# Sparse layer of a hybrid block: the key and value compression in halves between gate, value and query products, its second layer later, and the residual scaled inside the attention

## The chip, the cores and the metric

The kernel runs on one core of a Trainium2 chip. The metric is the device time of one execution in microseconds (us). Before the change it is 1653.73 us, the median of 3 runs (1653.6 to 1656.01).

## The reference

The program is a stack on 512 tokens of width 1024, all in float32. A first block (a pooling mixer and an mLSTM) ends with `rms_norm(h, norm_out_g)`. A second block of two layers follows. Its first layer is a sparse attention (NSA), the second a sliding-window attention; each is followed by a gated feed-forward part. The change lies in the sparse layer, after its input `h = rms_norm(x, norm_mix[0])`:

```python
q, kc, vc, ks, vs, kw, vw, gt = split(h @ w_in)     # 16 query heads, 4 key/value groups, head size 64
# q, kc, ks, kw are rotated (rope)
blk = (t[:, :, cidx] + pe).reshape(b, g, 31, 32 * 64)   # 31 overlapping blocks of 32 tokens
c   = gelu(blk @ w1) @ w2                               # compress: 2048 -> 256 -> 64, for kc and for vc
o_cmp = softmax(q @ compressed_keys) @ compressed_values
o_slc, o_win = attention on ks, vs and on kw, vw        # with 512 tokens both see all earlier tokens
o = gate0 * o_cmp + gate1 * o_slc + gate2 * o_win       # gates = sigmoid(gt + gate_b)
x = x + o @ w_o
```

The `x` of the last line is the output of the first block's norm, so it is the raw sum times a factor per token and a gain per feature; the kernel scales its residual tile `H` by both at some point before `w_o` adds to it.

## The kernel before

Activations lie transposed: features on the 128 partitions, 512 tokens along the free dimension, eight chunks for the width of 1024. `H` [128, 8, 512] holds the residual.

A float32 product is made of three matmuls in a faster 32-bit type. `split_into` and `unit` make of each operand a high half (a cast on ScalarE, ACT: `xh`, `wh`) and a low half (what is left, a subtraction on VectorE, DVE: `xl`, `wl`), and `mm3` multiplies high by high, high by low and low by high. `linear` takes one 512 KB piece of weights (128 output columns): `raw` loads it on the SyncE queue (SP) into one of three buffers `wr`, `unit` casts it (L120) and subtracts (L121) into one of three `wh` and three `wl`, and 8 x 3 matmuls (L126 to L128) fill one PSUM bank of 512 columns. The gate product has 48 output columns and 192 KB. The PSUM banks are two `mm`, three `S`, two `tp` and one `po`; with `wide=True` a product takes them in rotation, all but `tp`.

The compression's first layer is different: its weights come by `raw` too, eight pieces of 512 KB (four for keys, four for values), but are used in float32 as they are (L993). TensorE (PE) runs each of the 32 matmuls of one compression as two instructions on 124 columns, so the trace has 64.

The sparse layer (`nsa`) goes like this in program order:
1. the input is split, the first three products (`pre`) run beside the norm's sum of squares, and the rotation tables are scaled;
2. `cproj(0)` and `cproj(1)` evacuate the products for compressed keys and values (`cf`; keys are rotated), and `cmp_blocks` adds the position term into the block tiles `blk` (L981; per compression 12 additions on DVE and 4 on GpSimd, POOL);
3. `kproj(0)`: two key products, rotated by `rope` (a copy L601 on ACT, four small DMAs on SP that swap halves, `rot`, a product on POOL L606, a product and a sum on DVE L607, L608, into `kf`), then `dup_k`: scaled high and low halves and their copies into the other 64 partitions (L615 to L618, ACT and DVE);
4. `compress` of the keys: first layer L993 into two PSUM tiles, copies to `gx` on ACT (L998), the tanh form of gelu in five DVE instructions and one of ACT, second layer L1008 on PE, and two evacuations into `bd`; then `compress` of the values likewise, with the second layer L1015 and `vbd`;
5. `settle`: the norm's factor is broadcast over partitions (L190 on PE, a copy on ACT into `r1`), and eight DVE instructions (L817) scale `H` by it and by the gain;
6. `gate_proj`, `vproj(0)` (two products, evacuated to `vT`, transposed back by L644 in `v_nat`), `qproj(0)`, `cprobs(0)` (softmax on compressed keys), `qproj(1)`, `cvals(0)`;
7. the attention `att(fill)`: 32 steps, head pair p of 8 times query block j of 4. A step first runs what `fill` has for it (further projections, compressed softmax, output products), then the softmax of the step after (`nsa_soft`: scores on PE, maximum L929 or L938 on DVE, exponential L942 on ACT, and the scaling by the gates on DVE L955, POOL L953 and ACT L951), then the values of its own (`nsa_vals`: transposes L662, splits L148 and L149, products L666, L667).

The tiles `cf`, `kf`, `gt`, `vT`, `r1` and `qf` share two buffers of one tag ("kf"), so each waits until the one before the last is released.

The lines above give the program order. The framework (Tile) derives all waits from the tiles, and plans the order of each engine's queue before the run: of the instructions that its own estimate takes as ready, the one that is earliest in the program goes first. On the chip each engine, and SP with its DMA issues, then takes its queue strictly in that order.

Of the kernel before, what the change touches and what calls it, by code (L numbers as in the profile page):

```python
# [11 lines left out]
F32 = mybir.dt.float32  # L12
# [4 lines left out]
OP = mybir.AluOpType  # L17
# [4 lines left out]
T = 512  # L22
NT = 4
KC = 8
# [5 lines left out]
POOL_WINDOWS = (2, 4, 8, 16)  # L30

# [4 lines left out]
class Model:  # L36
    def __init__(self, ctx, tc, a, out):
# [4 lines left out]
        self.wpool = False  # L42
        con = self.con = ctx.enter_context(tc.tile_pool(name="con", bufs=1))
# [12 lines left out]
    def first_loads(self):  # L56
# [7 lines left out]
        r = self.wp.tile([128, 1024], F32, name=self.n("wr"), tag="wr", bufs=3)  # L64
# [39 lines left out]
    def wide_ps(self, shape=(128, 512)):  # L104

        self.rot_ps = (self.rot_ps + 1) % 6
        return (self.mm_ps, self.s_ps, self.s_ps, self.mm_ps, self.s_ps, self.o_ps)[self.rot_ps](shape)

    def raw(self, dram, i, cols=1024):
        r = self.wp.tile([128, 1024], F32, name=self.n("wr"), tag="wr", bufs=3)  # L110
        self.nc.sync.dma_start(r[:, :cols], dram[i])
        return r
# [572 lines left out]
    def nsa(self):  # L685
        tc, nc, a = self.tc, self.nc, self.a
        V, G, S, PE = nc.vector, nc.gpsimd, nc.scalar, nc.tensor
        with tc.tile_pool(name="nsa", bufs=1) as ap:
# [20 lines left out]
            X = {}  # L709
# [24 lines left out]
            def vproj(hf, wide=False):  # L734
                for b in range(2):
                    ps = self.linear(a["nsa_w"], 6 + 8 * hf + b, xh, xl, wide=wide)
                    vT = ap.tile([128, T], F32, name=self.n("vT"), tag="kf", bufs=2)
                    V.tensor_tensor(vT, ps, rb, op=OP.mult)
                    VV[b, hf] = self.v_nat(ap, vT, f"vn{b}", 1)

# [60 lines left out]
            def gate_proj():  # L801
# [3 lines left out]
                V.tensor_scalar(gt, gt, self.v("nsa_gate_b")[:48], None, op0=OP.add)  # L805
                gp = self.tp_ps([128, NT, 48])
# [4 lines left out]
                V.reciprocal(gn, gn)  # L811

            def settle():
                r1 = ap.tile([128, T], F32, name="r1", tag="kf", bufs=2)
                self.bcast(y1, r1)
                for k in range(KC):
                    V.scalar_tensor_tensor(self.H[:, k, :], self.H[:, k, :], self.v("norm_out_g", k), r1,  # L817
                                           op0=OP.mult, op1=OP.mult)

            bk = cproj(0)  # L820
            bv = cproj(1)
            kproj(0, True)
            self.compress(ap, 0, bk, w2, bd, vbd)
            self.compress(ap, 1, bv, w2, bd, vbd)
            settle()
            gate_proj()
            vproj(0, True)
            qproj(0, True)
            cprobs(0)
            qproj(1)  # L830
# [3 lines left out]
            add = lambda p, j, f, *x: fill.setdefault(4 * p + j, []).append(L(f, *x))  # L834
            add(0, 1, cprobs, 1)
# [13 lines left out]
            add(4, 0, vproj, 1)  # L849
# [134 lines left out]
    def compress(self, pool, kv, blk, w2, bd, vbd):  # L984
        nc, a = self.nc, self.a
        V, S, PE = nc.vector, nc.scalar, nc.tensor
        hps = [self.wide_ps([128, 124]) for _ in range(2)]
        for q in range(4):
            w = self.raw(a["cmp_w1"], 4 * kv + q)
            for jj in range(4):  # L990
                j = 4 * q + jj
                for m in range(2):
                    PE.matmul(hps[m], w[:, jj * 256 + m * 128:jj * 256 + m * 128 + 128], blk[j // 8][:, j % 8, :],  # L993
                              start=(j == 0), stop=(j == 15))
        x = pool.tile([128, 2, 124], F32, name=self.n("gx"), tag="pc", bufs=2)
        t = pool.tile([128, 2, 124], F32, name=self.n("gt_"), tag="pc", bufs=2)
        for m in range(2):
            S.copy(x[:, m], hps[m])  # L998
# [5 lines left out]
        V.tensor_scalar(x, x, 0.5, None, op0=OP.mult)  # L1004
        if kv == 0:
# [5 lines left out]
        else:  # L1011
# [5 lines left out]
            for h in range(2):  # L1017
                V.tensor_copy(vbd[32 * h:32 * h + 31, :, h * 64:h * 64 + 64], ps)

# [408 lines left out]
```

## Time and profile before

| | |
|---|---|
| median of 3 runs | 1653.73 us (1653.6 to 1656.01) |
| the profiled execution's own time | 1655.41 us |
| its span, first to last instruction | 1653.7 us, granted TensorE clock 0.992 |
| busy: PE, DVE, ACT, POOL | 1604.0, 1076.7, 790.6, 226.3 us |
| HBM read over the span | 130.50 MB, 80 GB/s |

The profile shows one execution. Busy times are the instructions' own durations; PE's are pipelined, and a matmul's end is modelled, so start-to-start times tell more than durations. "Granted clock" is the share of the full TensorE clock (2.4 GHz) that was granted; 0.50 is 1.2 GHz. In a timeline a row gives the start, the length and the group of instructions that follow each other; in brackets stands the idle time of the engine before it and what ended that. The sparse layer takes 384 to 750 us of the span; its part up to the first attention step ends near 488 us.

### The profile page before, as it was taken

The page shows a single profiled execution, that of the slowest core. Times are in us where ns is not written, and L with a number is a line of the kernel's source. Part 1 is how long each engine was busy: PE and PEld are TensorE (multiplying, and loading weights), DVE is VectorE, ACT ScalarE, POOL GpSimd, SP SyncE. Part 2 cuts the span into 40 slices and gives each one's busy share as a digit, 9 for nine tenths or more (in the row PEclk, how much of TensorE's full clock was granted, in tenths as well). Part 3 has the DMA queues.
Part 4 walks back from the last instruction along what each step waited for, and adds up shares of the span by engine and source line. Part 5 has one row for each costly group of instructions (what it writes and reads, how often), then busy time and mean ns, then how long its engine had stood idle before and what let it go on. Part 6 is the DMA issues. An engine that isn't in the chain of part 4 may idle for free.

```text
span 1653.7 us, 21346 instructions
## 1 busy us (share of the span) xinstructions
PE 1604.0 (97%) x7860; PEld 1302.9 (79%) x7860; DVE 1076.7 (65%) x1878; ACT 790.6 (48%) x1520; POOL 226.3 (14%) x294
## 2 busy tenths in 40 slices
PE   8999999999799999999999999998999999999998
PEld 6678888878677777777888888886777888888886
DVE  7677557766779999986555445357988655534532
ACT  5443265644248887764333233145876433323412
POOL 0000000142212212121111001013311111100100
PEclk9999999999899999999999999999999999999999
DMA  5222321133331111113323333233321323232321
GB/s 183 71 90 90 99 81 42 49 97 102 120 102 46 35 62 39 52 33 109 102 90 101 97 95 102 76 116 94 108 74 60 103 95 102 90 101 90 124 80 51
DMA packets 44792, 142.77 MB, mean 86 GB/s; under 512 B 6608, under 2 KB 6864, under 8 KB 44688
## 3 DMA queue, kind: packets, MB, share of 16 engines
q1 hardware_dynamic: 42384, 137.45, 26.7%
q10 hardware_dynamic: 2304, 3.96, 0.7%
q8 instruction: 62, 1.02, 0.3%
q14 instruction: 42, 0.34, 0.1%
HBM read 130.50 MB, written 2.10 MB: 80 GB/s over the span
## 4 chain that ended last, share of the span: by engine, by line
PE 81%; DVE 11%; ACT 4%; issue 3%; POOL 0%; DMA 0%; DVEq 0%; POOLq 0%; ACTq 0%
PE S L126 10%; PE S L128 10%; PE S L127 10%; PE mm L126 9%; PE mm L127 9%; PE mm L128 9%; PE po L126 3%; PE po L127 3%; PE po L128 3%; PE tp L662 2%; PE po L666 1%; PE po L667 1%; DVE wl L121 1%; DVE blk L981 1%; DVE ptl L149 1%
## 5 line engine op out<-in xcount | busy, mean ns | idle before, releaser
L120 ACT CAST wh<-wr 128x1024 fp32r<-128x1024 f32 (+1 forms) x224 | 233.1, 1043 | 486.4 <-PE S L127 208.4
L121 DVE TENSOR_TENSOR wl<-wr,wh 128x1024 fp32r<-128x1024 f32 (+1 forms) x215 | 264.6, 1231 | 51.2 <-ACT wh L120 35.9
L126 PE MATMUL mm<-xh,wh 128*128 128x512 f32 (+1 forms) x568 | 226.4, 399 | 0.7 <-ACT xh L148 0.4
L127 PE MATMUL mm<-xl,wh 128*128 128x512 f32 (+1 forms) x568 | 225.2, 396 | 0.5 <-DVE xl L152 0.5
L128 PE MATMUL mm<-xh,wl 128*128 128x512 f32 (+1 forms) x568 | 224.8, 396 | 0.0
L126 PE MATMUL S<-xh,wh 128*128 128x512 f32 x520 | 203.9, 392 | 7.1 <-ACT wh L69 6.4
L127 PE MATMUL S<-xl,wh 128*128 128x512 f32 x520 | 203.6, 392 | 0.7 <-DVE xl L152 0.5
L128 PE MATMUL S<-xh,wl 128*128 128x512 f32 x520 | 203.2, 391 | 0.2 <-DVE wl L121 0.2
L126 PEld LDWEIGHTS mm<-xh,wh 128*128 128x128 f32 (+1 forms) x568 | 106.8, 188 | 22.2 <-ACT xh L148 0.9
L127 PEld LDWEIGHTS mm<-xl,wh 128*128 128x128 f32 (+1 forms) x568 | 106.6, 188 | 22.1 <-DVE xl L152 1.2
L128 PEld LDWEIGHTS mm<-xh,wl 128*128 128x128 f32 (+1 forms) x568 | 106.6, 188 | 21.0 <-DVE wl L121 0.4
L126 PEld LDWEIGHTS S<-xh,wh 128*128 128x128 f32 x520 | 97.9, 188 | 28.2 <-ACT wh L69 6.4
L127 PEld LDWEIGHTS S<-xl,wh 128*128 128x128 f32 x520 | 98.0, 188 | 23.0 <-DVE xl L152 2.8
L128 PEld LDWEIGHTS S<-xh,wl 128*128 128x128 f32 x520 | 98.0, 189 | 21.2 <-DVE wl L121 1.3
L149 DVE TENSOR_TENSOR ptl<-tp,pth 128x512 fp32r<-128x512 f32 (+1 forms) x112 | 73.7, 664 | 7.0 <-ACT pth L148 6.2
L942 ACT ACTIVATE p<-S,nm 128x128 f32<-128x128 f32 (+3 forms) x128 | 67.3, 534 | 10.4 <-DVE nm L938 5.1
L148 ACT CAST pth<-tp 128x512 fp32r<-128x512 f32 (+1 forms) x112 | 63.3, 575 | 18.7 <-PE tp L662 15.9
L126 PE MATMUL po<-xh,wh 128*128 128x512 f32 x184 | 71.8, 390 | 0.0
L127 PE MATMUL po<-xl,wh 128*128 128x512 f32 x184 | 71.7, 390 | 0.0
L128 PE MATMUL po<-xh,wl 128*128 128x512 f32 x184 | 71.6, 389 | 0.0
L1201 POOL MEMSET fa<- 128x2 f32 x44 | 4.3, 100 | 450.6 <-DVE fc L1206 449.4
L1207 ACT ACTIVATE fc<-fc 128x512 f32<-128x512 f32 x44 | 27.9, 634 | 78.8 <-DVE fc L1206 78.8
(469 smaller groups left out, 3534.5 us busy)
## 6 DMA issues: line engine op xcount, KB each, us to landing
wr<-ffn_gu SPq DMA_DIRECT2D x88, 512.0 KB, 3.5
wr<-w_in SPq DMA_DIRECT2D x32, 512.0 KB, 3.7
wr<-ffn_d SPq DMA_DIRECT2D x32, 512.0 KB, 3.5
wr<-nsa_w SPq DMA_DIRECT2D x20, 512.0 KB, 3.6
wr<-w_out SPq DMA_DIRECT2D x16, 512.0 KB, 3.5
rot<-sq SPq DMA_DIRECT2D x92, 64.0 KB, 2.0
wr<-swa_w SPq DMA_DIRECT2D x10, 512.0 KB, 3.5
wr<-cmp_w SPq DMA_DIRECT2D x8, 512.0 KB, 4.2
```

Source lines behind the costliest of these rows:

```text
L120: nc.scalar.copy(h[:, :cols], r[:, :cols])
L121: (nc.gpsimd if self.wpool else nc.vector).tensor_tensor(l[:, :cols], r[:, :cols], h[:, :cols], op=OP.subtract)
L126: mm(ps, wh, xh, start=first, stop=False)
L127: mm(ps, wh, xl, start=False, stop=False)
L128: mm(ps, wl, xh, start=False, stop=last)
L148: nc.scalar.copy(h, src)
L149: nc.vector.tensor_tensor(l, src, h, op=OP.subtract)
L662: self.nc.tensor.transpose(ps[:, x, h, :], srcs[x][h], self.ident)
L666: self.nc.tensor.matmul(o, v, ph, start=first, stop=False)
L667: self.nc.tensor.matmul(o, v, pl, start=False, stop=last)
L942: S.activation(t[:, :w], sb[b], AF.Exp, bias=nm[:, 0, h, b:b + 1], accum_out=nm[:, 1, h, b:b + 1])
L1207: S.activation(c, c, AF.Silu)
```

## The change

- A fourth buffer for raw weights (`WR = 4`), everywhere in the kernel.
- In the sparse layer the rotation of wide PSUM banks leaves out `po` until the first `cprobs` (`self.banks = 5`).
- `compress` becomes a generator with a stop after each quarter of its first layer (16 of the trace's 64 instructions), after the gelu and after the second layer. Both column halves go into one `po` bank (one copy to `gx` instead of two), and `gx` and its scratch get a tag of their own.
- `vproj` does one product and is a generator (product and evacuation; transposes), `gate_proj` too (product and evacuation; transposes and sigmoid).
- They are advanced in this order: two key quarters, gate product, two key quarters with gelu, value product 0, gate transposes, two value quarters, value product 1, transposes of 0, two value quarters with gelu, second layer for keys, query product 0, transposes of 1, broadcast of `r1`, query product 1, second layer for values, then `cprobs(0)` and `cvals(0)`.
- `settle` scales one chunk of `H`, as a multiplication by the gain on ACT and one by `r1` on POOL. The eight calls stand in `fill` at the steps j = 1 and 3 of head pairs 0 to 3. `r1` has its own tile.
- The later `vproj(1)` is advanced as product, product, transposes, transposes in step (4, 0).

```diff
+WR = 4
...
     def wide_ps(self, shape=(128, 512)):
 
-        self.rot_ps = (self.rot_ps + 1) % 6
+        self.rot_ps = (self.rot_ps + 1) % self.banks
...
     def raw(self, dram, i, cols=1024):
-        r = self.wp.tile([128, 1024], F32, name=self.n("wr"), tag="wr", bufs=3)
+        r = self.wp.tile([128, 1024], F32, name=self.n("wr"), tag="wr", bufs=WR)
...
-            X = {}
+            self.banks = 5
...
-            def vproj(hf, wide=False):
-                for b in range(2):
+            def vproj(hf, b, wide=False):
+                if True:
                     ps = self.linear(a["nsa_w"], 6 + 8 * hf + b, xh, xl, wide=wide)
                     vT = ap.tile([128, T], F32, name=self.n("vT"), tag="kf", bufs=2)
                     V.tensor_tensor(vT, ps, rb, op=OP.mult)
+                    yield
                     VV[b, hf] = self.v_nat(ap, vT, f"vn{b}", 1)
+                    yield
...
                 V.tensor_scalar(gt, gt, self.v("nsa_gate_b")[:48], None, op0=OP.add)
+                yield
                 gp = self.tp_ps([128, NT, 48])
...
-            def settle():
-                r1 = ap.tile([128, T], F32, name="r1", tag="kf", bufs=2)
-                self.bcast(y1, r1)
-                for k in range(KC):
-                    V.scalar_tensor_tensor(self.H[:, k, :], self.H[:, k, :], self.v("norm_out_g", k), r1,
-                                           op0=OP.mult, op1=OP.mult)
+                yield
+
+            def settle(k):
+                S.mul(self.H[:, k, :], self.H[:, k, :], self.v("norm_out_g", k))
+                G.tensor_tensor(self.H[:, k, :], self.H[:, k, :], r1, op=OP.mult)
 
             bk = cproj(0)
             bv = cproj(1)
             kproj(0, True)
-            self.compress(ap, 0, bk, w2, bd, vbd)
-            self.compress(ap, 1, bv, w2, bd, vbd)
-            settle()
-            gate_proj()
-            vproj(0, True)
+            ck = self.compress(ap, 0, bk, w2, bd, vbd)
+            cv = self.compress(ap, 1, bv, w2, bd, vbd)
+            gt = gate_proj()
+            v0, v1 = [vproj(0, b, True) for b in range(2)]
+            next(ck)
+            next(ck)
+            next(gt)
+            next(ck)
+            next(ck)
+            next(v0)
+            next(gt)
+            next(cv)
+            next(cv)
+            next(v1)
+            next(v0)
+            next(cv)
+            next(cv)
+            next(ck)
             qproj(0, True)
+            next(v1)
+            r1 = ap.tile([128, T], F32, name="r1")
+            self.bcast(y1, r1)
+            qproj(1, True)
+            next(cv)
+            self.banks = 6
             cprobs(0)
-            qproj(1)
             cvals(0)
...
+            for k in range(KC):
+                add(k // 2, 1 + 2 * (k % 2), settle, k)
...
-            add(4, 0, vproj, 1)
+            v2, v3 = [vproj(1, b) for b in range(2)]
+            for g in (v2, v3, v2, v3):
+                add(4, 0, next, g)
...
     def compress(self, pool, kv, blk, w2, bd, vbd):
         nc, a = self.nc, self.a
         V, S, PE = nc.vector, nc.scalar, nc.tensor
-        hps = [self.wide_ps([128, 124]) for _ in range(2)]
+        hps = self.o_ps([128, 2, 124])
         for q in range(4):
             w = self.raw(a["cmp_w1"], 4 * kv + q)
             for jj in range(4):
                 j = 4 * q + jj
                 for m in range(2):
-                    PE.matmul(hps[m], w[:, jj * 256 + m * 128:jj * 256 + m * 128 + 128], blk[j // 8][:, j % 8, :],
-                              start=(j == 0), stop=(j == 15))
-        x = pool.tile([128, 2, 124], F32, name=self.n("gx"), tag="pc", bufs=2)
-        t = pool.tile([128, 2, 124], F32, name=self.n("gt_"), tag="pc", bufs=2)
-        for m in range(2):
-            S.copy(x[:, m], hps[m])
+                    PE.matmul(hps[:, m], w[:, jj * 256 + m * 128:jj * 256 + m * 128 + 128], blk[j // 8][:, j % 8, :],
+                              start=(j == 0 and m == 0), stop=(j == 15 and m == 1))
+            if q < 3:
+                yield
+        x, t = [pool.tile([128, 2, 128], F32, name=self.n(s), tag="gx", bufs=2)[:, :, 0:124] for s in ("gx", "gt_")]
+        S.copy(x, hps)
...
         V.tensor_scalar(x, x, 0.5, None, op0=OP.mult)
+        yield
...
                 V.tensor_copy(vbd[32 * h:32 * h + 31, :, h * 64:h * 64 + 64], ps)
+        yield
```

## Rows read from the trace of the kernel before

**Rows 1.** The page's first part: busy us of each engine, its share of the span and its instructions.

```profile
PE 1604.0 (97%) x7860; PEld 1302.9 (79%) x7860; DVE 1076.7 (65%) x1878; ACT 790.6 (48%) x1520; POOL 226.3 (14%) x294
```

**Rows 2.** Busy time by stretch: from and to in us, length, busy us of PE, PEld (its weight loads), DVE, ACT and POOL with instructions in brackets, granted clock, DMA share, GB/s.

```profile
405.00:420.00 15.00, 15.00 (x72) 12.55 (x71) 12.14 (x16) 2.23 (x3) 6.19 (x6) 1.00 0.27 79
420.00:450.00 30.00, 20.50 (x139) 19.15 (x138) 21.07 (x34) 8.78 (x17) 5.92 (x6) 0.84 0.35 113
450.00:480.00 30.00, 29.88 (x157) 22.99 (x157) 20.49 (x30) 10.77 (x15) 0.00 (x0) 0.99 0.44 140
...
560.00:610.00 50.00, 49.28 (x293) 38.77 (x292) 48.60 (x99) 42.38 (x104) 12.04 (x14) 1.00 0.23 69
```

**Rows 3.** Timeline of PE from 423 to 460 us: start, length, line, result and operands, count, and the wait before it.

```profile
423.70 0.38 PE L993 MATMUL po<-blk,wr 128*128 128x124 f32 x2
...
430.96 0.48 PE L993 MATMUL po<-blk,wr 128*128 128x124 f32 x2 [1.75 <-DMA wr<-cmp_w]
...
433.02 3.83 PE L993 MATMUL S<-blk,wr 128*128 128x124 f32 x32
437.94 0.46 PE L993 MATMUL S<-blk,wr 128*128 128x124 f32 x2 [1.09 <-DMA wr<-cmp_w]
445.05 1.19 PE L1008 MATMUL tp<-gx,w 128*128 128x124 f32 x4 [6.65 <-DVE gx L1004]
446.03 5.78 PE L993 MATMUL S<-blk,wr 128*128 128x124 f32 x30
451.57 0.47 PE L126 MATMUL mm<-xh,wh 128*48 128x512 f32 x1
...
454.70 1.05 PE L1015 MATMUL tp<-w,gx 128*31 128x64 f32 x16
455.68 1.16 PE L190 MATMUL tp<-ident,nwy 128*128 128x128 f32 x8
...
459.46 0.39 PE L126 MATMUL S<-xh,wh 128*128 128x512 f32 x1
```

**Rows 4.** Busy time in stretches of 2 us, columns as in rows 2; the granted clock is the number after POOL.

```profile
439.00:441.00 2.00, 0.00 (x0) 0.00 (x0) 1.37 (x2) 1.94 (x4) 0.00 (x0) 0.88 0.12 44
...
447.00:449.00 2.00, 2.00 (x11) 2.00 (x11) 0.45 (x1) 0.00 (x0) 0.00 (x0) 0.50 0.00 0
449.00:451.00 2.00, 2.00 (x13) 2.00 (x12) 0.00 (x0) 0.00 (x0) 0.00 (x0) 0.56 0.32 63
```

**Rows 5.** Timeline of DVE from 413 to 447 us.

```profile
413.69 8.26 DVE L981 TENSOR_TENSOR blk<-cf,pe 64x248 f32<-64x248 f32 x12
...
423.19 9.78 DVE L981 TENSOR_TENSOR blk<-cf,pe 64x248 f32<-64x248 f32 x12
...
434.20 0.68 DVE L608 TENSOR_TENSOR kf<-kf,rot 128x512 f32<-128x512 f32 x1
435.58 1.40 DVE L616 SCALAR_TENSOR_TENSOR kd<-kf,kd 64x512 fp32r<-64x512 f32 x2 [0.70 <-ACT kd L615]
...
439.21 1.41 DVE L616 SCALAR_TENSOR_TENSOR kd<-kf,kd 64x512 fp32r<-64x512 f32 x2 [1.50 <-ACT kd L615]
```

**Rows 6.** Timeline of ACT from 434 to 443 us.

```profile
434.92 1.28 ACT L615 ACTIVATE kd<-kf 64x512 fp32r<-64x512 f32 x2 [10.39 <-DVE kf L608]
...
441.54 0.61 ACT L618 CAST kd<-kd 64x512 fp32r<-64x512 f32 x1
442.05 0.25 ACT L998 COPY gx<-po 128x124 f32<-128x124 f32 x1
```

**Rows 7.** Timeline of SP's DMA issues (weights of the compression and of the gate product), then, from the page's list of issues, KB each and the median us to landing.

```profile
405.05 4.04 SPq L111 DMA_DIRECT2D wr<-cmp_w  x2
...
436.88 0.33 SPq L111 DMA_DIRECT2D wr<-nsa_g  x1
...
wr<-cmp_w SPq DMA_DIRECT2D x8, 512.0 KB, 4.2
```

**Rows 8.** The eight scalings of `H`: durations in ns (least, median, greatest), first and last start; then the nearest rows for the two operations that take their place, from the groups by line and form within 480 to 760 us: count, busy us, mean ns.

```profile
L817 DVE SCALAR_TENSOR_TENSOR H<-H,vec,r x8: 746/748/748, 458.0 to 462.7; 128x512 f32<-128x512 f32 x8
...
L606 POOL TENSOR_TENSOR rot<-rot,sin 128x512 f32<-128x512 f32 x10 | 13.2, 1323 | 66.3 <-DMA rot<-sq 66.3
...
L951 ACT ACTIVATE p<-p,nm 128x512 f32<-128x512 f32 x8 | 5.9, 732 | 2.1 <-DVE nm L946 2.1
```

**Rows 9.** What PE waited for between 480 and 760 us: us in total, times, longest.

```profile
PE tp L902 <- POOL pc L893: 1.1, 2, 0.6
PE po L667 <- DVE ptl L149: 1.1, 4, 0.4
```

**Rows 10.** Timeline of DVE, then of POOL, between 537 and 542 us.

```profile
538.02 0.68 DVE L149 TENSOR_TENSOR ptl<-tp,pth 128x512 fp32r<-128x512 f32 x1
...
540.27 1.24 DVE L955 TENSOR_SCALAR p<-p,nm 128x512 f32<-128x512 f32 x1
...
541.43 0.47 DVE L955 TENSOR_SCALAR p<-p,nm 128x512 f32<-128x512 f32 x1
...
537.70 1.30 POOL L606 TENSOR_TENSOR rot<-rot,sin 128x512 f32<-128x512 f32 x1 [2.36 <-DMA rot<-sq]
540.19 1.04 POOL L953 TENSOR_TENSOR p<-p,nm 128x512 f32<-128x512 f32 x1 [1.19 <-DVE nm L946]
```

**Rows 11.** What PE waited for in the whole run: the longest row on weights that were not yet cast (the first product's, L69, left out).

```profile
PE S L126 <- ACT wh L120: 0.7, 1, 0.7
```

More of the change, by code (lines that the diff above doesn't have):

```diff
@@ L104, in wide_ps @@
     def wide_ps(self, shape=(128, 512)):
-        self.rot_ps = (self.rot_ps + 1) % 6
+        self.rot_ps = (self.rot_ps + 1) % self.banks
         return (self.mm_ps, self.s_ps, self.s_ps, self.mm_ps, self.s_ps, self.o_ps)[self.rot_ps](shape)
     def raw(self, dram, i, cols=1024):
-        r = self.wp.tile([128, 1024], F32, name=self.n("wr"), tag="wr", bufs=3)
+        r = self.wp.tile([128, 1024], F32, name=self.n("wr"), tag="wr", bufs=WR)
         self.nc.sync.dma_start(r[:, :cols], dram[i])
@@ L822, in nsa @@
             kproj(0, True)
-            self.compress(ap, 0, bk, w2, bd, vbd)
-            self.compress(ap, 1, bv, w2, bd, vbd)
-            settle()
-            gate_proj()
-            vproj(0, True)
-            qproj(0, True)
+            ck = self.compress(ap, 0, bk, w2, bd, vbd)
[16 more added lines that the diff above has]
+            next(ck)
+            qproj(0, True)
+            next(v1)
[3 more added lines that the diff above has]
+            next(cv)
+            self.banks = 6
             cprobs(0)
-            qproj(1)
             cvals(0)
```

## The prediction

> **What bounds the kernel now.** I read the page first: TensorE (PE) is busy for 97% of the span [rows 1], so only places where PE stands still, or runs at the lower of its two clocks, can give time back. The busy time by stretch finds the one such place that this change touches: 405 to 420 us is full, 420 to 450 us has 20.50 of 30 us at a mean granted clock of 0.84, and from 450 us on PE is full again [rows 2]. The timeline of PE shows what it waited for there: 1.75 us and 1.09 us for compression weights still in transfer, and 6.65 us for the hidden layer of the first compression (gx), 9.5 us in all [rows 3]. The long one also costs clock: the grant falls to 0.50 (1.2 GHz) at about 440.5 us (0.88 as the mean of 439 to 441) and is back near 450.75 us, some 5.7 us after PE went on [rows 4]. In that time thirty compression matmuls took 5.78 us, 0.19 each, where 32 took 3.83 us, 0.12 each, at full clock [rows 3]; that is 2.2 us, and the four L1008 matmuls, 1.19 us for what four such steps do in 0.5, add 0.7. So the stretch loses 12.4 us, 0.75% of the span.
>
> Who is late is in the timelines of VectorE (DVE) and ScalarE (ACT). DVE works from 413.69 to 434.88 us with no pause: two times twelve block additions (8.26 and 9.78 us) with two evacuations between, and only then the rotated keys kf [rows 5]. ACT waits 10.39 us for those, does the key copies from 434.92 to 442.15, and only then reads gx at 442.05 [rows 6]. The chain is additions, keys, key copies, gx; PE's order decides how much of it lies beside PE work. The order in each engine's queue is set before the run, by program order and by the planner's estimate of what is ready: 34 matmuls of the second compression stand ahead of L1008, which comes earlier in the program [rows 3]. It expected gx 34 matmuls after the first compression; on the chip it came 12 us after. Its estimate of DVE and ACT is too fast here, and I expect that of the new order too.
>
> **The change, part by part.** The sum runs from the end of the key products, 423.70 us, to the start of the first value product, 459.46 us [rows 3].
>
> *Order of PE.* Before, this held both compressions (128 matmuls), L1008, the gate product, L1015, one broadcast (L190), 9.5 us of waits and 2.9 us of lost clock. Afterwards only the first compression and the gate product stand there; 64 compression matmuls (64 x 0.12 = 7.4 us at most, 7.2 by 0.112 from start to start), L1008 (0.45), L1015 (1.05) and L190 (1.05 to 1.16) come later, between value and query products: 9.8 us moved, none removed.
>
> *Does PE still stand?* Two quarters of the compression take it to 423.7 + 3.6 = 427.3 us; their inputs and weights are there (two weight loads issued at 405.05 us [rows 7]). Then comes the gate product. With four buffers its weights no longer queue behind the compression's (issued 436.88 us [rows 7]) but take the third place of the loads from 405 us. Its high half can be cast on ACT, which is idle between its copies [rows 6]. Its low half (wl, 0.56 us) is DVE work, and in the program behind the additions and the keys; DVE has no pause before 434.88 us, where it waits 0.70 us for ACT [rows 5]. The planner puts ready work into such a pause. So I take wl as done at 434.9 us; the bounds are 422 us (put between the two dozens of additions) and 440.6 us (behind the last key copy of DVE, 439.21 + 1.41 [rows 5]). The third matmul of the gate product needs it, and PE takes its instructions in order: it stands from 427.7 to 434.9, 7.2 us. Behind it in PE's queue are the rest of the compression and the value product, and behind these gx. The clock falls as it did before; 5.7 us at half speed from 434.9 cost 2.9 us, the same as now. The rest of the gate product is 22 x 0.23 = 5.1 us (451.57 to 459.46 less 2.15 for L1015 and L190, over 24 [rows 3]), the other two quarters 3.6. The first value product starts at 434.9 + 5.1 + 3.6 + 2.9 = 446.5 us; with the 9.8 us still to do this compares with 456.3 against 459.5: **-3.2 us**. Value weights would be no earlier help: their high half stands among ACT's key copies, which end at 442.15, plus 1.05 for the cast and 1.23 for the low half give 444.4. So even a gate product that waits for nothing would leave PE waiting at the value product, at nearly the same total.
>
> *Later.* From there each late result has a product of over 5 us before its use: gx of the first compression is due after four products, the second compression finds its blocks (done 432.97 us [rows 5]). The shared po bank makes it wait for the copy of gx, covered by the first value product. Loads issued one product ahead have 4.2 us to land [rows 7]. I take 0, bounds 0 to +2.5 (another wait like the 1.75 and 1.09).
>
> *Residual scaling.* Eight DVE instructions of 0.748 us go [rows 8], but they lay beside a full PE [rows 2]: nothing gained. In their place stand eight ACT multiplies (0.73 us by the nearest, L951) and eight POOL products (1.32 us by L606) [rows 8] in pairs 0 to 3 of the attention, where DVE has 48.60 and ACT 42.38 of 50 us and PE waits for others only 1 us or so per line [rows 2, 9]. Each is queued ahead of softmax work on its engine, which the transposes on PE wait for. POOL also slows DVE: an L955 on 512 columns takes 1.24 us beside POOL's L953, and the next one, alone, 0.47: 0.77 us more [rows 10]. Bounds: -0.5 (all covered, some DVE relief before) to 8 x 1.32 = +10.6; I take **+1.5**, near the lower end since the planner has other matmuls to put there and PE's waits are short.
> The Trainium skill (GPSIMD Engine Reference, Key points) says that GpSimd shares its SBUF interfaces with VectorE and contends with its instructions in a 2-port mode or with two SBUF inputs. By it the low halves read from PSUM are spared, and L149 beside L606 does take 0.68 us [rows 10]; so a stretch of 0.77 x 8 = 6.2 us of DVE, if every product met such an instruction, becomes perhaps half of that. The rows alone would allow the whole.
>
> *Fourth weight buffer elsewhere.* The longest row of PE's waits for cast weights, after the first product, is 0.7 us in the whole run [rows 11]: nearly nothing to gain directly; a new planned order may shift short waits, bounds -2 to +2, taken as 0. The smaller tiles (r1, gx) cost nothing, and one POOL or ACT instruction less or more beside a full PE costs nothing either.
>
> **Sum.** -3.2 + 1.5 = -1.7 us. The profiled execution took 1655.41 us, 1.7 around its span of 1653.7; it would take 1653.7. It lies 1.7 above the median of the runs, 1653.73, so I expect 1652.0 us; own range 1649 to 1656.
>
> **The rivals.**
> *Nothing waits* (24%): the planner slips the low half of the gate weights between the additions and the value weights ahead of the key copies. For it: ACT's idle 10.39 us, weights early. Against: DVE without a pause [rows 5, 6]. All 12.4 us go: 1653.7 - 12.4 + 1.5 = 1642.8 us.
> *The attention pays* (16%, ends slower): in pairs 0 to 3 the POOL product stands ahead of POOL's own softmax scale and PE's transposes wait for it, 1.32 us each time: 1653.7 - 3.2 + 10.6 = 1661.1 us. For it: DVE at 97% there [rows 2]. Against: short PE waits [rows 9]. It decides from (3.2 + 3.3) / 8 = 0.8 us for each.
> *The gate product is held to the end of the key copies* (7%, slower): wl at 440.6, 5.7 us later: 1653.7 - 3.2 + 5.7 + 1.5 = 1657.7 us.
> *It does not do what it says* (7%): the planner sees the gate weights late and puts compression matmuls first, as now; only the scaling changes: 1655.2 us.
>
> **How the numbers follow.** My forecast has 46%. A measurement here tells 0.2%, 3.3 us, from no change. Faster: the first rival and 16 of the forecast's 46, 40%. Same: 27 of the 46, the last rival and a mild case of the second, 38%. Slower: 3 of the 46, the second and third, 22%. The range goes from under the first rival, 1641.5, to past the third, 1659.
>
> **What would show it.** Right: PE stands 6 to 8 us before the third gate matmul, released by DVE wl; clock 0.50 for some 6 us after; no long wait before L1008. Wrong: PE full from 423.7 to 460 us (then 1643), or PE waits for POOL's p in pairs 0 to 3 that sum to over 5 us (then slower).

## The result and the profile after

The changed kernel takes 1664.33 us (median of 4 runs, 1663.12 to 1664.83), the kernel before 1653.78 beside it: 1.0054 times as long, 95% interval 1.0042 to 1.0067, so 10.5 us slower. The prediction was 1652.0 us, faster, with a range up to 1659.

All line numbers of the sparse layer are larger now: L111 is L113, L120 and L121 are L122 and L123, L126 to L128 are L128 to L130, L149 is L151, L594 is L596, L606 and L608 are L608 and L610, L662 and L667 are L664 and L669, L882 is L907, L953 and L955 are L978 and L980, L981 is L1006, L993 is L1018, L1008 is L1034, L1015 is L1041. The page's first part, to hold against [rows 1]:

```profile
PE 1609.8 (97%) x7860; PEld 1304.6 (78%) x7860; DVE 1069.0 (64%) x1870; ACT 792.0 (48%) x1526; POOL 233.7 (14%) x302
```

PE has some 6 us more of busy time in a span 9.1 us longer. Busy time by stretch (columns as in [rows 2]):

```profile
405.00:420.00 15.00, 15.00 (x72) 12.55 (x71) 10.50 (x12) 2.24 (x4) 6.21 (x6) 1.00 0.24 67
420.00:450.00 30.00, 22.76 (x123) 17.03 (x122) 23.47 (x38) 9.54 (x16) 5.97 (x6) 0.88 0.30 90
450.00:480.00 30.00, 30.00 (x171) 25.84 (x170) 13.84 (x21) 10.08 (x14) 2.18 (x2) 0.95 0.55 182
480.00:510.00 30.00, 23.48 (x130) 17.87 (x129) 17.80 (x41) 14.76 (x40) 13.11 (x14) 0.89 0.20 64
560.00:610.00 50.00, 49.15 (x289) 37.66 (x289) 46.36 (x101) 42.73 (x106) 12.53 (x14) 1.00 0.20 59
```

The known hole in 420 to 450 us has shrunk, from 20.50 to 22.76 busy us, and a second one has opened: 23.48 of 30 us from 480 us on, where PE was full but for 1.4 us before. The timeline of PE shows both (two stretches of it; [rows 3] are the rows of before):

```profile
426.27 3.73 PE L1018 MATMUL po<-blk,wr 128*128 128x124 f32 x32
...
435.73 0.66 PE L130 MATMUL S<-xh,wl 128*48 128x512 f32 x1 [5.26 <-DVE wl L123]
...
442.50 3.73 PE L1018 MATMUL po<-blk,wr 128*128 128x124 f32 x32
447.68 0.50 PE L128 MATMUL S<-xh,wh 128*128 128x512 f32 x1 [1.45 <-ACT wh L122]
...
448.94 0.50 PE L130 MATMUL S<-xh,wl 128*128 128x512 f32 x1 [0.52 <-DVE wl L123]
...
482.14 1.08 PE L1041 MATMUL tp<-w,gx 128*31 128x64 f32 x16
489.74 1.97 PE L907 MATMUL tp<-bd,qf 128*128 128x64 f32 x8 [6.52 <-DVE qf L610]
491.47 0.77 PE L128 MATMUL mm<-xh,wh 128*128 128x512 f32 x1
```

The first wait, 5.26 us in the gate product for the low half of its weights, was forecast. The two short ones at value 0, 1.45 and 0.52 us, were not: the sum had both halves of the value weights at 444.4 us, ahead of their product. The timelines of SP, POOL and ACT show where they were held up:

```profile
435.70 0.33 SPq L113 DMA_DIRECT2D wr<-cmp_w  x1
436.14 2.40 SPq L596 DMA_DIRECT2D rot<-sq  x4
...
440.90 1.31 POOL L608 TENSOR_TENSOR rot<-rot,sin 128x512 f32<-128x512 f32 x1 [10.62 <-DMA rot<-sq]
...
446.59 1.04 ACT L122 CAST wh<-wr 128x1024 fp32r<-128x1024 f32 x1
```

SP stood 11.5 us at a compression load whose buffer came free only with the gate's low half. The swap of the second key's halves, ready to go since 427.1 us, stands behind that load in SP's queue. So the key copies on ACT end at 446.6 us, 1.8 us later than before if both are counted from the end of the key products, and the value weights are cast only then. PE, which had stood less at the gate than forecast, was there first.

The long wait, 6.52 us, is that of the compressed scores of query 0 (L907) for its rotated tile qf (L610). The timeline of DVE, first at the gate ([rows 5] before), then at query 0:

```profile
425.78 8.70 DVE L1006 TENSOR_TENSOR blk<-cf,pe 64x248 f32<-64x248 f32 x12
434.52 0.69 DVE L609 TENSOR_TENSOR kf<-S,cos 128x512 f32<-128x512 f32 x1
435.12 0.55 DVE L123 TENSOR_TENSOR wl<-wr,wh 128x384 fp32r<-128x384 f32 x1
...
489.00 0.69 DVE L610 TENSOR_TENSOR qf<-qf,rot 128x512 f32<-128x512 f32 x1 [10.13 <-POOL rot L608]
489.60 1.22 DVE L123 TENSOR_TENSOR wl<-wr,wh 128x1024 fp32r<-128x1024 f32 x1
```

The gate's wl is done at 435.7 us, right behind the dozen of block additions and one key instruction; the forecast was 434.9, in a trace that is 2.6 us earlier here. At 489.00 us DVE itself had waited 10.13 us, for POOL. The timeline of POOL:

```profile
477.82 9.92 POOL L821 TENSOR_TENSOR H<-H,r 128x512 f32<-128x512 f32 x8 [35.62 <-ACT r L195]
487.70 1.26 POOL L608 TENSOR_TENSOR rot<-rot,sin 128x512 f32<-128x512 f32 x1
```

Here is the cause, which the experiments below test. All eight products of the residual with r1 run in one block of 9.92 us from the moment that ACT has r1, and query 0's rotation (L608) stands behind them. The change wrote the products into steps of head pairs 0 to 3, which begin about 494 us. But nothing they read is later than r1, and POOL had nothing else to do then, so the planner put them all ahead. The eight ACT multiplies went further still, to 394.5 us. After the wait comes the clock, by stretch:

```profile
483.00:490.00 7.00, 0.48 (x5) 0.32 (x4) 1.00 (x2) 0.39 (x2) 5.96 (x5) 0.80 0.00 0
490.00:492.00 2.00, 2.00 (x9) 1.95 (x10) 1.94 (x3) 1.54 (x3) 0.00 (x0) 0.50 0.07 25
492.00:494.00 2.00, 2.00 (x6) 1.57 (x5) 1.92 (x5) 0.00 (x0) 0.00 (x0) 0.50 0.79 273
494.00:496.00 2.00, 2.00 (x15) 1.56 (x15) 1.28 (x5) 0.81 (x4) 0.49 (x1) 0.99 0.32 95
```

The grant is 0.50 from 490 to 494 us: 1.2 GHz after PE had stood, and 2 us more lost. Between 480 and 760 us nothing else is to be seen in PE's waits (us, times, longest), beside [rows 9]:

```profile
PE tp L907 <- DVE qf L610: 6.5, 1, 6.5
PE po L669 <- DVE ptl L151: 1.2, 3, 0.5
```

### The profile page after: what moved, and what is told of

It reads as the page before. It is cut to its first block, busy times and chain, and to the rows that moved or that the text cites. A ratio compares the mean times of both kernels' runs of the same rounds, so it can differ in the third digit from the quotient of the medians.

```text
span 1662.8 us, 21345 instructions
## 1 busy us (share of the span) xinstructions
PE 1609.8 (97%) x7860; PEld 1304.6 (78%) x7860; DVE 1069.0 (64%) x1870; ACT 792.0 (48%) x1526; POOL 233.7 (14%) x302
## 4 chain that ended last, share of the span: by engine, by line
PE 80%; DVE 10%; ACT 5%; issue 3%; POOL 1%; DMA 0%; SPq 0%; DVEq 0%; ACTq 0%; POOLq 0%
PE S L130 10%; PE S L128 10%; PE S L129 10%; PE mm L128 9%; PE mm L129 9%; PE mm L130 8%; PE po L128 3%; PE po L130 3%; PE po L129 3%; PE tp L664 2%; PE po L668 1%; PE po L669 1%; DVE wl L123 1%; DVE blk L1006 1%; ACT p L967 1%
## 5 line engine op out<-in xcount | busy, mean ns | idle before, releaser
L122 ACT CAST wh<-wr 128x1024 fp32r<-128x1024 f32 (+1 forms) x224 | 232.9, 1041 | 485.9 <-PE S L129 216.6
L123 DVE TENSOR_TENSOR wl<-wr,wh 128x1024 fp32r<-128x1024 f32 (+1 forms) x215 | 263.1, 1224 | 55.7 <-ACT wh L122 40.3
L128 PE MATMUL mm<-xh,wh 128*128 128x512 f32 x568 | 227.1, 400 | 0.8 <-ACT xh L150 0.5
L129 PE MATMUL mm<-xl,wh 128*128 128x512 f32 x568 | 225.2, 397 | 0.5 <-DVE xl L154 0.5
L130 PE MATMUL mm<-xh,wl 128*128 128x512 f32 x568 | 225.2, 396 | 0.0
L128 PE MATMUL S<-xh,wh 128*128 128x512 f32 (+1 forms) x536 | 212.0, 395 | 9.2 <-ACT wh L71 7.1
L130 PE MATMUL S<-xh,wl 128*128 128x512 f32 (+1 forms) x536 | 211.3, 394 | 6.0 <-DVE wl L123 6.0
L129 PE MATMUL S<-xl,wh 128*128 128x512 f32 (+1 forms) x536 | 211.3, 394 | 0.3 <-DVE xl L154 0.2
L128 PEld LDWEIGHTS S<-xh,wh 128*128 128x128 f32 (+1 forms) x536 | 101.3, 189 | 31.8 <-ACT wh L71 7.1
L129 PEld LDWEIGHTS mm<-xl,wh 128*128 128x128 f32 x568 | 107.6, 189 | 21.9 <-DVE xl L154 1.2
L128 PEld LDWEIGHTS mm<-xh,wh 128*128 128x128 f32 x568 | 107.7, 190 | 21.6 <-ACT xh L150 1.0
L130 PEld LDWEIGHTS S<-xh,wl 128*128 128x128 f32 (+1 forms) x536 | 101.2, 189 | 29.6 <-DVE wl L123 8.0
L130 PEld LDWEIGHTS mm<-xh,wl 128*128 128x128 f32 x568 | 107.6, 189 | 21.5 <-DVE wl L123 0.4
L151 DVE TENSOR_TENSOR ptl<-tp,pth 128x512 fp32r<-128x512 f32 (+1 forms) x112 | 73.3, 663 | 7.2 <-ACT pth L150 6.2
L967 ACT ACTIVATE p<-S,nm 128x128 f32<-128x128 f32 (+3 forms) x128 | 67.0, 531 | 15.9 <-DVE nm L954 10.8
L128 PE MATMUL po<-xh,wh 128*128 128x512 f32 x168 | 65.4, 390 | 0.0
L130 PE MATMUL po<-xh,wl 128*128 128x512 f32 x168 | 65.4, 389 | 0.0
```

The costliest lines, as they stand in the source:

```text
L122: nc.scalar.copy(h[:, :cols], r[:, :cols])
L123: (nc.gpsimd if self.wpool else nc.vector).tensor_tensor(l[:, :cols], r[:, :cols], h[:, :cols], op=OP.subtract)
L128: mm(ps, wh, xh, start=first, stop=False)
L129: mm(ps, wh, xl, start=False, stop=False)
L130: mm(ps, wl, xh, start=False, stop=last)
L151: nc.vector.tensor_tensor(l, src, h, op=OP.subtract)
```

## The experiments

A ratio is always to the kernel before, in runs beside it, with its 95% interval; medians of the kernel before in these sets are 1654.7 to 1655.8 us. My theory (T1) after the two profiles: the front gains what was forecast, and the block of products ahead of query 0's rotation takes more than that back.

**Products held in place.** POOL's order alone changes; the queues of the other four engines stay word for word.

```diff
-                G.tensor_tensor(self.H[:, k, :], self.H[:, k, :], r1, op=OP.mult)
+                self.tc.keep_in_program_order(G.tensor_tensor(self.H[:, k, :], self.H[:, k, :], r1, op=OP.mult))
```

> The changed kernel with the eight POOL products of the residual held at their places in the program (the queues of PE, DVE, ACT and SP stay as they are; only POOL's order differs). Theory T1, the eight products run as one block of 9.9 us ahead of query 0's rotation and PE stands 6.7 us for it, plus some 3 us of clock: the stall at 483 us is gone and the time falls by 7 to 10 us, to 1654 to 1657. Rival A, POOL's products cost the attention wherever they stand: no gain, 1662 to 1668, with PE waiting for POOL's softmax scale in pairs 0 to 3. Rival C, the new order of the front itself (no query 2 product at hand as filler) makes the stall: 1663 to 1665 and PE still stands over 4 us near 483 us.

Measured: 1660.6 us, 1.0032 (1.0019 to 1.0044). The stall at 483 us is gone, so it was the block's; that refutes rival C. But only 3.7 us came back, about half of what T1 expected at least, since now the attention pays, as rival A has it. What PE waited for between 480 and 760 us:

```profile
PE po L669 <- DVE ptl L151: 4.0, 5, 1.5
PE tp L664 <- DVE p L980: 1.0, 2, 0.7
```

POOL's own softmax scale is not among them. It is DVE that is late: two groups by line and form from 510 to 660 us (count, busy us, mean ns), first in the changed kernel, then in this one:

```profile
L151 DVE TENSOR_TENSOR ptl<-tp,pth 128x512 fp32r<-128x512 f32 x50 | 33.6, 682 | 2.7 <-ACT pth L150 2.2
...
L980 DVE TENSOR_SCALAR p<-p,nm 128x512 f32<-128x512 f32 x10 | 7.4, 768 | 0.0
```

```profile
L151 DVE TENSOR_TENSOR ptl<-tp,pth 128x512 fp32r<-128x512 f32 x48 | 32.2, 682 | 2.8 <-ACT pth L150 2.3
...
L980 DVE TENSOR_SCALAR p<-p,nm 128x512 f32<-128x512 f32 x10 | 11.5, 1177 | 0.0
```

L980, from SBUF to SBUF, takes 1177 ns in place of 768; L151, which reads PSUM, keeps its 682. One such place, in the timelines of POOL, DVE and PE of this run:

```profile
569.03 1.04 POOL L978 TENSOR_TENSOR p<-p,nm 128x512 f32<-128x512 f32 x1 [5.37 <-ACT wh L122]
570.03 1.45 POOL L821 TENSOR_TENSOR H<-H,r 128x512 f32<-128x512 f32 x1
...
569.11 2.66 DVE L980 TENSOR_SCALAR p<-p,nm 128x512 f32<-128x512 f32 x2
...
573.89 0.38 PE L669 MATMUL po<-ptl,vn 128*128 128x256 f32 x1 [1.01 <-DVE ptl L151]
```

Two L980 beside POOL's scale and product take 2.66 us, and PE then waits for ptl, which stands behind them on DVE. After that wait the clock falls too; the grant is 0.61 from 574 to 576 us, and then:

```profile
576.00:578.00 2.00, 2.00 (x8) 1.53 (x7) 1.68 (x3) 1.79 (x6) 0.00 (x0) 0.54 0.52 156
```

PE's waits on the two rows are 5.0 us against 1.5 in the changed kernel, and the clock costs 1.7 us: 5.2 of the some 7 us by which the table below has the attention longer. The rest is not traced to a cause.

**One part alone, on the kernel before.** First the fourth weight buffer, then the scaling (with `settle(k)` as in the change).

```diff
-        r = self.wp.tile([128, 1024], F32, name=self.n("wr"), tag="wr", bufs=3)
+        r = self.wp.tile([128, 1024], F32, name=self.n("wr"), tag="wr", bufs=4)
```

```diff
-            settle()
+            r1 = ap.tile([128, T], F32, name="r1")
+            self.bcast(y1, r1)
...
+            for k in range(KC):
+                add(k // 2, 1 + 2 * (k % 2), settle, k)
```

> The kernel before with the fourth weight buffer alone. T1: 1655.5 to 1657 (2 to 3 us slower). Rival B: 1660 or more. Nothing: 1653.5 to 1654.

> The kernel before with the scaling alone: eight ACT multiplies and eight POOL products in steps of pairs 0 to 3, r1 in a tile of its own, its broadcast where it was. The planner again puts all eight products in one block ahead of query 0's rotation, but r1 is there some 20 us sooner. T1: the block is done before the rotation is due, so 1653 to 1655. Rival A (eight products cost wherever they stand): 1660 or more.

Measured: 1654.54 us, 0.9998 (0.9988 to 1.0007), and 1654.5, 0.9999 (0.9991 to 1.0008): each nothing. In the second, the eight products run in one block ahead of query 0's rotation too, but r1's broadcast is inside the gate product there, and the block, begun at 456.61 us, has been done for 12.84 us when the rotation starts. So a block alone doesn't cost; what decides is when it may begin.

**Three buffers in the changed kernel.**

```diff
-WR = 4
+WR = 3
```

> The changed kernel with three weight buffers again. By T1 the fourth buffer costs the 2.6 us that the two profiles are apart by the end of the last key product, and no more: 1661 to 1663. Rival B, the buffer is the main cost (rotations of keys and query 0 wait on SP behind one more weight load): 1654 to 1657. If the 2.6 us are chance between two profiles: 1664.

Measured: 1662.17 us, 1.0041 (1.0029 to 1.0054). That is at most a small part of the loss, and the interval overlaps that of the changed kernel. The 2.6 us by which the two profiles were apart at the end of the key products were there before the sparse layer. At the last residual addition ahead of it, the traces of the nine other runs with four buffers are 0.5 to 1.5 us behind the kernel before, and the three with three buffers within 0.2: about 1 us goes with the buffer there, and the rest of the 2.6 is that one execution's. Alone, the buffer costs the run nothing.

**The broadcast of r1 sooner.** Two lines move, nothing else.

```diff
             next(v0)
             next(gt)
+            r1 = ap.tile([128, T], F32, name="r1")
+            self.bcast(y1, r1)
             next(cv)
...
             next(v1)
-            r1 = ap.tile([128, T], F32, name="r1")
-            self.bcast(y1, r1)
             qproj(1, True)
```

> The changed kernel with the broadcast of r1 moved ahead: behind the gate transposes instead of behind query 0's product, some 20 us earlier. The planner again puts all eight POOL products in one block ahead of query 0's rotation. T1, now with a price of place (held in pairs 0 to 3 the products cost the attention some 0.8 us each; as one block they cost only what the rotation behind them is late): the block ends before the rotation is due, the 9.3 us that the stall at 483 us adds go, 1654 to 1657. Rival C (the front leaves no filler ahead of query 0's scores, so that PE stands there anyway): 1660 or more. Rival D (POOL's block beside DVE's copies of the value tiles slows DVE, and PE waits for it): 1658 to 1660.

Measured: 1651.91 us, 0.9974 (0.9965 to 0.9983). The two moved lines are worth 0.8%, some 13 us, and turn a loss into a gain; with that, rivals C and D are out. It is more than T1 had, too: of what the table below gives back, 9.4 us are the stall, and some 3.5 in the front and the attention T1 does not explain. POOL's block in the timeline:

```profile
454.25 11.92 POOL L821 TENSOR_TENSOR H<-H,r 128x512 f32<-128x512 f32 x8 [14.18 <-ACT r L195]
```

The stretch from 480 us:

```profile
480.00:510.00 30.00, 29.99 (x169) 22.55 (x168) 28.27 (x64) 22.24 (x61) 8.11 (x10) 1.00 0.20 54
```

The block is longer (11.92 us), but query 0's rotation is not due yet when it ends, and PE is full.

**The scaling undone, the rest kept**, with that early broadcast.

```diff
-                S.mul(self.H[:, k, :], self.H[:, k, :], self.v("norm_out_g", k))
-                G.tensor_tensor(self.H[:, k, :], self.H[:, k, :], r1, op=OP.mult)
+                V.scalar_tensor_tensor(self.H[:, k, :], self.H[:, k, :], self.v("norm_out_g", k), r1,
+                                       op0=OP.mult, op1=OP.mult)
...
             self.bcast(y1, r1)
+            for k in range(KC):
+                settle(k)
...
-            for k in range(KC):
-                add(k // 2, 1 + 2 * (k % 2), settle, k)
```

> The changed kernel without its scaling part: eight DVE instructions right behind the early broadcast, as in the kernel before; what is left is the new order of the front and the fourth buffer. T1: the front's gain of 2.8 us less 0 to 2.6 for the buffer and 0 to 2.5 that the attention lost in the changed kernel without POOL's products: 1651 to 1656, and within 2 us of the run with the early broadcast. If the order itself costs the attention what the first run of this study lost there: 1658 or more.

Measured: 1652.07 us, 0.9979 (0.9971 to 0.9988). New order and buffer, with the early broadcast, gain 0.2%, some 3.5 us; the forecast's term was 3.2. Whether the products run on POOL early or on DVE makes no difference that the runs show.

To see where the time of each kernel goes, I take of each trace the stretch from the last residual addition of the stage before to the first of the attention. Each has the same 1446 matmuls there. The table sums what the distance from one matmul's start to the next is over a full-speed distance (from the lower fifth of all distances of that form; another choice of it moves whole columns, and the 9.3 us below by up to some 2), by equal work: the first 60 us of work (to the value products), the next 20 (to query 0's scores), and the rest of 208 us. One profiled execution of each:

| kernel | first 60 | next 20 | rest |
|---|---|---|---|
| before | 15.4 | 1.2 | 37.7 |
| changed | 12.6 | 10.5 | 38.7 |
| products held in place | 12.7 | 1.9 | 45.3 |
| broadcast sooner | 11.5 | 1.1 | 36.3 |
| scaling undone | 13.3 | 1.1 | 37.4 |

The front gains 2.8 us; the block costs 9.3, of which 6.52 of wait and 2 of clock stand in the rows above; products in place cost the attention 7 more than the block does there. For the changed kernel that makes 7.4 us in this stretch; with the 2.6 before it, and some 0.8 given back after it, its span is 9.1 longer. Small differences here are not sure: a profiled execution lies up to some 2 us from the median of its kernel, and one with the buffer alone, which the runs give nothing, passes this stretch in 258.4 us where the kernel before takes 262.0.

**Can the front's own waits go?** Next, the order first compression, gate, second compression, value 0, with the early broadcast (the calls on one line here); then the same with `WR = 3`.

```diff
-   ck ck gt ck ck v0 gt bcast cv cv v1 v0 cv cv ck q0 v1 q1 cv
+   ck ck ck ck gt cv cv cv cv v0 gt bcast ck v1 v0 q0 v1 cv q1
```

> The changed kernel in another order of the front: the whole first compression, gate, the whole second compression, and only then value 0, with the early broadcast. My theory of the gate stall (PE stands 5.4 us for the gate's low half, which DVE brings at 435.7, and 2.3 us for the value weights at 446.6 to 447.6): 32 more compression matmuls (3.7 us) stand ahead of the gate product and 32 more ahead of the value product, so PE waits at most 2 us at each; some 5 us and most of the 2.9 of clock come back: 1646 to 1651. If the stalls only move to the second compression (its weights, or the bank po waiting for gx): 1654 to 1657.

> The same order with three weight buffers. If the fourth buffer is worth nothing here: the same within 1.5 us as the run before. If compression weights come late without it, as in the kernel before (waits of 1.75 and 1.09 us): 2 to 4 us slower than the run before.

Measured: 1653.97 us, 0.999 (0.9981 to 0.9999), and 1657.79, 1.0014 (1.0006 to 1.0023). My theory failed here. The timeline of PE of the first:

```profile
425.24 7.30 PE L1018 MATMUL po<-blk,wr 128*128 128x124 f32 x64
440.57 0.66 PE L128 MATMUL S<-xh,wh 128*48 128x512 f32 x1 [8.03 <-ACT wh L122]
```

With a later gate product the planner cast its high half later, between ACT's key copies, and PE waited 8.03 us for that. The buffer is worth 3.8 us in this order: without it a compression weight was 1.82 us late in transfer, and PE waited 9.27 us for the bank po, until ACT had copied gx out of it.

**Gate weights loaded and split sooner**, in the change's order, then in the new one (there with the last line too).

```diff
-                ps = self.linear(a["nsa_g"], 0, xh, xl, m=48, wide=True)
+                ps = self.linear(a["nsa_g"], 0, xh, xl, m=48, wide=True, pre=gw)
...
             bk = cproj(0)
+            gw = self.unit(a["nsa_g"], 0, KC * 48)
             bv = cproj(1)
...
-        hps = self.o_ps([128, 2, 124])
+        hps = (self.tp_ps if kv else self.o_ps)([128, 2, 124])
```

> The changed kernel with the early broadcast, and the gate weights loaded and split ahead of the key and block work, so that the gate product has both halves when PE reaches it; the order of PE is kept. The prediction's claim: a gate product that waits for nothing would leave PE waiting at the value product, whose weights are split behind the key copies, at nearly the same total. By it the 5.2 us wait at the gate goes and one of 6 to 10 us at value 0 comes: within 2 us of the run with the early broadcast, 1650 to 1654. Rival: the value weights come sooner too, as ACT and DVE are rid of the gate's split at 435 us, and the 5 us and the clock come back: 1643 to 1648.

> The same early gate weights, in the order first compression, gate, second compression, value 0, with the second compression's sums in a bank of the transposes' pair, so that it doesn't wait for gx. Theory: the 8.0 us wait for the gate's high half that this order showed goes, PE has 7.4 us of compression, 5.5 of gate and 7.4 of compression from 426.5 us on, up to 446.8, and the value weights are there at about 446: no wait over 2 us, and no 5.7 us of half clock: 8 to 11 us faster than that order with the late weights, 1643 to 1646. If the second compression's inputs or weights are late (four loads behind four buffers), a wait of 3 to 6 us there: 1648 to 1652.

Measured: 1654.74 us, 0.9997 (0.9988 to 1.0006), and 1656.53, 1.0008 (0.9999 to 1.0018): both slower than forecast, the second by over 10 us. The gate's load took the place of the second key product's, and that product now waits for its low half behind the same additions. PE in the second of them:

```profile
434.65 0.80 PE L130 MATMUL mm<-xh,wl 128*128 128x512 f32 x1 [5.15 <-DVE wl L123]
```

**The low half on POOL.** The gate weights are loaded behind the second key product's, and POOL, idle between its block additions, makes the low half; again in both orders.

```diff
                     ps = self.linear(a["nsa_w"], 4 + 8 * hf + b, xh, xl, wide=wide)
+                    if wide and b == 1:
+                        self.wpool = True
+                        gw.extend(self.unit(a["nsa_g"], 0, KC * 48))
+                        self.wpool = False
```

> The changed kernel with the early broadcast, and the gate weights loaded behind the second key product's and their low half made on POOL, which is idle between its block additions, instead of on DVE; the order of PE is kept. The prediction's claim, again: the 5.2 us wait at the gate goes and one of 6 to 10 us at value 0 comes (its high half is cast behind the key copies, at 444 to 445 us), so the time stays within 2 us of the run with the early broadcast, 1650 to 1654. Rival: the value weights come sooner too and the stall goes: 1643 to 1648.

> The same gate weights in the order first compression, gate, second compression (its sums in a bank of the transposes' pair), value 0. Theory: everything PE meets between 426.5 and 446.8 us is there (the gate's halves from 415 to 423, blocks from 433, compression weights a buffer ahead), and the value weights at 446 to 447.5: no wait over 2 us and no half clock after it, some 9 to 11 us of the 12.4 come back: 1643 to 1647 against 1654 before. If the value weights still are late by the loads' queue (their buffer comes free with the second compression's first quarter, 4 us to land): 1647 to 1651. If a wait of the old length only moves: 1653 to 1656.

Measured in the change's order: 1652.14 us, 0.9982 (0.9973 to 0.9991), the same as with the gate's wait. POOL's split, and PE's wait in its place:

```profile
417.75 1.12 POOL L123 TENSOR_TENSOR wl<-wr,wh 128x384 fp32r<-128x384 f32 x1
...
444.50 0.80 PE L128 MATMUL S<-xh,wh 128*128 128x512 f32 x1 [7.46 <-ACT wh L122]
```

The stretches after it, the granted clock being the number after POOL:

```profile
444.00:446.00 2.00, 1.46 (x3) 0.74 (x4) 1.52 (x2) 0.71 (x2) 0.00 (x0) 0.50 0.00 0
...
448.00:450.00 2.00, 2.00 (x6) 1.55 (x5) 0.03 (x1) 0.66 (x1) 0.00 (x0) 0.50 0.98 401
450.00:452.00 2.00, 2.00 (x9) 1.62 (x9) 1.22 (x1) 1.67 (x2) 0.00 (x0) 0.95 0.02 6
```

The gate waits for nothing, and the value product waits 7.46 us for its high half, behind the key copies; the grant is 0.50 until 450 us. In the new order: 1649.39 us, 0.9964 (0.9952 to 0.9977), the lowest median of all and faster than both kernels (its interval overlaps that of the early broadcast alone). PE's two waits there:

```profile
446.83 0.50 PE L128 MATMUL S<-xh,wh 128*128 128x512 f32 x1 [2.04 <-ACT wh L122]
...
448.91 0.50 PE L130 MATMUL S<-xh,wl 128*128 128x512 f32 x1 [1.35 <-DVE wl L123]
```

The clock in that stretch:

```profile
440.00:444.00 4.00, 4.00 (x38) 4.00 (x38) 1.37 (x2) 3.90 (x8) 0.00 (x0) 1.00 0.78 200
444.00:450.00 6.00, 2.61 (x15) 1.80 (x14) 5.18 (x10) 3.67 (x6) 0.00 (x0) 1.00 0.66 223
450.00:454.00 4.00, 4.00 (x19) 3.15 (x17) 1.12 (x1) 0.00 (x0) 0.00 (x0) 1.00 0.89 303
```

Both compressions now lie beside additions and key copies. In the table's terms the first 60 us of work carry 6.0 us, where the kernel before has 15.4. But the runs gain 0.36%, some 6 us, and the forecast of 1643 to 1647 is missed: the profiled execution is the fastest of the five (1647.55 us, mean grant 0.996; the others 1649.35 to 1651.31 at 0.992 to 0.995), and PE still stands 3.4 us at value 0. It isn't the loads' queue that is late there: the weights had landed at 442.96 us, and their cast, at 445.74, stands on ACT behind the key copies and the first gelu.

## Why the prediction was wrong

*What bounds the kernel, and does PE still stand?* Right in the place and near in the sum, but not in its parts. PE stood at the third gate matmul, released by DVE wl, 5.3 us instead of 7.2, and at value 0, where no wait was forecast, 2.0 us. The grant was 0.50 twice, from 435.7 to about 439.4 and from about 449.7 to 453.1 us, 3.6 us lost. Together that is 10.8 us against the forecast's 7.2 and 2.9; that it came out near is in part luck. For the value weights the prediction had asked what stands ahead of them on ACT and DVE, but not what stands ahead of the second key's swap on SP. Order and buffer gain some 3.5 us in the runs (with the early broadcast) against a term of 3.2. The claim that a gate product with no wait would only move it to value 0 held: 7.46 us there, 1652.14 against 1651.91 us. So the first rival, a gain of 12 us with nothing waiting, could not come from the gate weights alone.

*Later.* This step failed. It said that each late result has a product of over 5 us before its use, and gave 0 to +2.5 us. Query 0's rotation did have query 1's product before its use, but in POOL's queue it had 9.92 us of products before it. PE stood 6.52 us for it and lost 2 us of clock; by the table the term, taken as 0, is 9.3 us.

*Residual scaling.* The error behind it: I placed the eight products in the steps where the program has them, and priced them there at +1.5. On the gate I had written that the planner puts ready work into a pause, and I applied that to the gate's low half and not to products that need only r1, nor asked what POOL had next once r1 was there. [rows 8 to 10] price an instruction; none of them says where the planner puts it.

*The attention pays* (16%) came nearest with 1661.1 us, but for another reason than happened. Tried by itself, its size was good: products held in place are 0.53% (1.0032 less 0.9979), some 9 us, slower than with the scaling undone, where the rival had 10.6. So my +1.5 was some 7 us too low even for the place that I priced. The rival's mechanism was not what happened: the waits that the trace shows are for DVE, which POOL slows, not for POOL. The Trainium skill (GPSIMD Engine Reference, Key points) says that GpSimd contends with DVE instructions in a 2-port mode or with two SBUF inputs. The traces agree as far as they go: 1177 against 768 ns from SBUF to SBUF, no change where one input is PSUM; in which mode L980 runs, they don't show.

*Fourth weight buffer.* Right at 0 alone (0.9998); in a better order it is worth 3.8 us.

*The sum.* With the broadcast two products sooner the changed kernel takes 1651.9 us, and my sum was 1652.0. That is luck: the kernel before took 1655.8 us beside it, so the gain is some 4 us where the sum had 1.7, and the sum held 1.5 us for products in the attention that now run ahead of it. The parts come to -3.5 us (order with buffer, with the early broadcast) and 0 (scaling alone), and together they gave +10.5: the loss was in the meeting of two of them, the late broadcast and the moved products, and no term of mine was for that.

## What to carry to other kernels

Where a planner orders the queues, work written into a later step runs as soon as its inputs are there; ask of each moved instruction when its last input comes, what its engine has next at that time, and who waits for that. A long block of work with no hurry needs either an early input, so that it ends before its engine is wanted, or a hold in program order, and the hold has its own price on a neighbour. A DMA queue is no different: a load that waits for its buffer holds up the small transfers behind it. When a wait has several late results behind it, mending one shows the next (gate, then value weights): order and supplies had to change together for a gain.

## What was not expected of the hardware

The length of a pause did not tell by itself whether the clock falls. Pauses of 5.26, 6.52, 7.46 and 8.03 us took the grant to 0.50, for some 4 us after 6.52 us at 489.74 and some 5.7 us after 7.46 us at 444.50. In the last run's profiled execution a pause of 2.04 us followed by one of 1.35 us left it at 1.00. But in the changed kernel 1.45 and 0.52 us at value 0, 12 us after the gate's long wait, were followed by 0.50:

```profile
450.00:452.00 2.00, 2.00 (x7) 1.51 (x6) 0.71 (x2) 0.41 (x1) 0.00 (x0) 0.50 0.73 289
```

And with the products held in place the grant fell to 0.61 and 0.54 (574 to 578 us) after a pause of 1.01 us. What decides, these runs don't show.

POOL's products took longer in company too: 1.27 us (median of the eight) as a block beside a DVE that waited, 1.40 in the attention.
